# Rotary halves in separate chunks, scores of four heads in 32-row groups, and q and k by 512-column operands

## The chip, the cores and the metric

The kernel runs on one core of a Trainium2 chip. The metric is the device time of one execution in microseconds (us). The engines are PE (TensorE), ACT (ScalarE), DVE (VectorE), POOL (GpSimd) and SP, which issues the DMAs. PEld is the weight-load half of PE, which overlaps its matmuls.

## What is computed

Two layers of a decoder trunk on x of 256 tokens by 1024 channels. Each layer has three causal branches (a gated convolution of 31 taps, differential attention, block attention with one block), gates, an output projection, a layer norm and a squared-ReLU MLP. What the change touches is the rotary step and the scores of the two attentions:

```
u = x @ w_in[l]                                   # q and k of both attentions are column blocks of it
def apply_rope(x, cos, sin):                      # per head, 64 channels = two halves of 32
    x1, x2 = split(x, 2, axis=-1)
    return x * cos + concatenate([-x2, x1]) * sin
s = einsum("qd,kd->qk", q, k) * 64 ** -0.5        # per head; 8 heads in each attention, causal mask, softmax
```

The gates (`sigmoid(u_gate + b_gate)`) and the convolution (`conv_general_dilated` over 512 channels) run around these steps and share their engines.

## The kernel before

Every float32 operand is split in a high and a low float32r part, and a product is the sum of high by high, low by high and high by low. Weights come from HBM in **slabs** of 128 x 1024. For a slab, `Weights.get` (line 395) records a DMA into `raw`, a cast to `whi` on ACT and a subtraction that gives `wlo` on DVE; 4 raw and 8 whi/wlo buffers go round. x lies in `big` tiles, 256 columns of high and 256 of low part side by side, so that `x_both` is one 512-column operand.

A slab of the transposed projections holds 8 K chunks of 128 x 128 (`KT` = 8) and makes one chunk of 128 output channels over 256 tokens. There are two ways to multiply it:

- `tunit` (line 555; gates, and the MLP's first matrix with `hsplit`): for each K chunk one matmul of `whi` with the 512 columns of high and low x, then for each K chunk one of `wlo` with the 256 high columns. That is 8 matmuls of 512 and 8 of 256 columns. The two halves of the bank are then added by `tsum`: ACT copies the right half with the bias, DVE adds the left one.
- `qkunit` (line 575; q and k): `mm3` makes three matmuls of 256 columns for each K chunk, 24 for a slab, and two slabs fill one PSUM bank.

`rope` (line 655) takes such a bank: ACT makes four copies of 32 partitions that swap the halves of each head, DVE multiplies by cos, multiplies the swapped copy by a signed sin, and adds: three DVE instructions of 128 x 512. q or k of two slabs, which is four heads, is one unit; there are four q/k pairs of units in a layer (2 attentions by 2), 16 slabs, and 32 in the two layers.

`attn_scores` (line 675) makes the scores of two heads: for each head one matmul of 256 and one of 128 columns (the causal part) on 64 partitions, in float32, then mask and minimum on DVE and the exponential on ACT. It runs 8 times in a layer. Stages `d_a` to `d_d` (differential) and `m_a` to `m_c` (block attention) follow; `tick()` starts them after a given number of slabs.

PSUM has 8 banks (`BANKS`, line 30): 2 `pm` (projections), 4 `pa` (scores, transposes and products of the attention, layer norm), 2 `pt` (the second slab of `tunit`, some transposes).

The convolution is 124 **taps** in a layer, each one DVE instruction of 128 x 256 (`tap`, line 618; in the profile `big<-hpad,half,big`). All of them have to be done before `conv_ln` (line 810) transposes their sum on PE, in the third gate group.

The order on each engine comes from `Plan`: every operation is recorded with a cost, dependences and a latest time (`latest`, line 234), and `order` (line 286) then takes at each step the operation that can start first on its engine, and of those ready the one with the earliest latest time. Line 125 is the line in `record` that issues everything, so all groups in the profile carry it and are told apart by tile names. Taps have late times and fill the gaps on DVE.

Of the kernel before, what the change touches and what calls it, by code (L numbers as in the profile page):

```python
# [9 lines left out]
F32 = mybir.dt.float32  # L10
F32R = mybir.dt.float32r
AF = mybir.ActivationFunctionType
# [29 lines left out]
class Plan:  # L42
# [68 lines left out]
    def record(self, name, fn, method, args, kw):  # L111
# [253 lines left out]
def kernel(ctx: ExitStack, tc: tile.TileContext, x, xT, w_in, w_p2, w_o, w_f1, w_f2,  # L365
# [165 lines left out]
    for l in range(L):  # L531
# [23 lines left out]
        def tunit(ticks=True):  # L555
            out = []
            for c in range(2):
                w = W.get(k=KT)
                ps = bank(("pm", "pt")[c])
# [7 lines left out]
                if ticks:  # L567
                    tick()
            return out

        def tsum(dst, ps, bias):

            R.Activation.activation(dst, ps[:, SEQ:], AF.Identity, bias=bias)
            R.DVE.tensor_add(dst, dst, ps[:, 0:SEQ])

        def qkunit():
            ps = bank()
            for c in range(2):
                w = W.get(k=KT)
# [3 lines left out]
                tick()  # L583
            return ps
# [69 lines left out]

        def rope(ps, dst):
            qq = R.tile(work, [P, 1024], F32, "zz", 3)
            q, qr = qq[:, :512], qq[:, 512:]
            for a in range(0, P, 64):
                R.Activation.copy(qr[a:a + 32], ps[a + 32:a + 64])
                R.Activation.copy(qr[a + 32:a + 64], ps[a:a + 32])  # L660
            p3 = ps.rearrange("p (c n) -> p c n", c=2)
            q3 = q.rearrange("p (c n) -> p c n", c=2)
            qr3 = qr.rearrange("p (c n) -> p c n", c=2)
            cb = cosT.rearrange("p (o n) -> p o n", o=1).broadcast_to([P, 2, SEQ])
            sb = sinT.rearrange("p (o n) -> p o n", o=1).broadcast_to([P, 2, SEQ])
# [7 lines left out]
        def attn_scores(b, pair):  # L673

            q, k = [QK[b, w, pair // 2][:, pair % 2] for w in 'qk']
            pt = R.tile(work, [P, 2, 384], F32, "pt", 2)
            mn = col(4, "mn")
            ll = col(4, "ll")
            li = col(4, "li")
            for e in range(2):  # L680
# [4 lines left out]
                for (s, m, j) in ((slice(0, 256), slice(0, 256), 2 * e),  # L685
                                  (slice(256, 384), slice(128, 256), 2 * e + 1)):
                    R.DVE.tensor_tensor_reduce(
                        out=pt[:, e, s], in0=ps[:, s], in1=maskq[:, m], scale=-0.125,
                        scalar=3.0e38, op0=ALU.add, op1=ALU.min, accum_out=mn[:, j:j + 1])
                    R.Activation.activation(pt[:, e, s], pt[:, e, s], AF.Exp, bias=mn[:, j:j + 1],  # L690
                                         scale=-1.0, accum_out=ll[:, j:j + 1])
            R.DVE.reciprocal(li, ll)
            return pt, ll, li

        def transp(src):

            ps = bank("pa")
# [15 lines left out]
        def d_a(h):  # L713
            pt, ll, li = attn_scores(0, h)
# [17 lines left out]
        def d_c(h):  # L732
            t, li = state['d', h]
            ps = bank("pa")
# [18 lines left out]
        def d_d(h):  # L753
            o = state['d', h]
            ps = bank("pa")
# [5 lines left out]
        def m_a(j):  # L761
            pt, ll, li = attn_scores(1, j)
# [14 lines left out]
        def m_c(j):  # L777
            t = state['m', j]
            t = t.rearrange("p (e n) -> p e n", e=2)
            ps = bank("pa")  # L780
# [10 lines left out]
        jobs = [[lambda f=f, h=h: f(h) for f in (d_a, d_b, d_c, d_d)] for h in range(4)]  # L791
        jobs += [[lambda f=f, h=h: f(h) for f in (m_a, m_b, m_c)] for h in range(4)]
        start = [7, 9, 11, 14, 16, 18, 20, 22]
        ev = []
        for i, (j, s) in enumerate(zip(jobs, start)):
            for k, f in enumerate(j):
                ev.append((s + 3 * k, -k, i, f))
# [186 lines left out]
        for i in range(3, 16):  # L984
            do2(i - 3)
            ps = tunit()
# [24 lines left out]
def _layout(x, w_in, b_gate, conv_w, conv_b, conv_ln_g, conv_ln_b, w_conv_out,  # L1011
# [21 lines left out]
    for l in range(L):  # L1033
# [3 lines left out]
        for q, k in ((dq, dk), (mq, mk)):  # L1037
            a, b = tu(q), tu(k)
# [25 lines left out]
    sinT = np.concatenate([-s, s, -s, s])  # L1064
# [29 lines left out]
```

## Time and profile before

| | |
|---|---|
| median of 3 runs | 856.26 us (855.24 to 857.37) |
| the profiled execution's own time | 855.5 us |
| its span in the trace | 853.7 us |
| busy share: PE, DVE, ACT | 98%, 77%, 64% |
| mean granted PE clock | 0.996 |

The span goes from the first to the last instruction of the core; the 1.8 us between it and the execution's own time lie around it. A matmul's end in the trace is modelled and overlaps the next one, so times of PE are read from start to start. In the same way a DVE or ACT instruction overlaps the next by some 0.08 us; the time that one takes from a full queue is its start-to-start time.

### The profile page before, as it was taken

The numbers are of one execution on the slowest core, as the hardware profiler recorded it, in microseconds if no ns is written. First come the engines' busy times: TensorE is split into PE (matmuls) and PEld (weight loads), VectorE is DVE, ScalarE is ACT, GpSimd is POOL, SyncE is SP. The second block draws the span as 40 slices with busy tenths as digits, with TensorE's granted clock in tenths as the row PEclk, the third lists the DMA queues.
The fourth block names the chain that finished last, engine by engine and source line by source line (L and its number), as shares of the span: only waits on it lengthen the run. The fifth ranks groups of instructions, "written<-read, shape, count | busy, mean of one in ns | idle before, by whom it ended". The sixth has DMA issues, their size and how long they took to land.

```text
span 853.7 us, 13190 instructions
## 1 busy us (share of the span) xinstructions
PE 840.0 (98%) x4938; PEld 737.5 (86%) x4938; DVE 655.4 (77%) x1123; ACT 543.6 (64%) x916; POOL 18.0 (2%) x26
## 2 busy tenths in 40 slices
PE   9999999999999999999999999999999999999996
PEld 7899988889888888888888998898898788888885
DVE  6789999998797655555679999999787875555545
ACT  6568998557258666656454799966662586666650
POOL 0000010000000000000000001000000000000000
PEclk9999999999999999999999999999999999999999
DMA  9775424555548765555275743355643586565511
GB/s 342 284 249 166 138 89 136 196 187 188 194 148 271 272 197 194 179 194 195 77 233 176 241 152 113 102 172 171 202 163 129 207 301 214 193 196 197 195 52 50
DMA packets 44415, 156.95 MB, mean 184 GB/s; under 512 B 4928, under 2 KB 5696, under 8 KB 44352
## 3 DMA queue, kind: packets, MB, share of 16 engines
q1 hardware_dynamic: 43920, 155.60, 54.5%
q8 instruction: 38, 0.62, 0.3%
q10 hardware_dynamic: 432, 0.52, 0.2%
q14 instruction: 25, 0.20, 0.1%
HBM read 155.06 MB, written 1.05 MB: 183 GB/s over the span
## 4 chain that ended last, share of the span: by engine, by line
PE 88%; ACT 5%; DVE 4%; issue 1%; DMA 0%; POOL 0%; DVEq 0%; ACTq 0%
PE pm L125 41%; PE pa L125 31%; PE pt L125 16%; ACT zz L125 2%; DVE wlo L125 1%; ACT pt L125 1%; DVE big L125 1%; DVE zz L125 1%; ACT o L125 1%; DVE pt L125 1%; ACT whi L125 1%; DMA zz<-in_xT_dram 0%; DVE qk L125 0%; DVE col L125 0%; POOL col L125 0%
## 5 line engine op out<-in xcount | busy, mean ns | idle before, releaser
L125 DVE TENSOR_TENSOR wlo<-raw,whi 128x1024 fp32r<-128x1024 f32 (+1 forms) x282 | 341.0, 1214 | 135.6 <-ACT whi L125 133.9
L125 ACT CAST whi<-raw 128x1024 fp32r<-128x1024 f32 (+1 forms) x282 | 293.3, 1046 | 172.5 <-PE pm L125 56.2
L125 PE MATMUL pm<-big,whi 128*128 128x256 f32 (+1 forms) x1296 | 270.1, 320 | 0.0
L125 PEld LDWEIGHTS pm<-big,whi 128*128 128x128 f32 x1296 | 215.2, 191 | 17.2 <-DVE big L125 0.7
L125 PE MATMUL pa<-whi,big 128*128 128x512 f32 x704 | 217.6, 391 | 0.6 <-ACT whi L125 0.6
L125 PE MATMUL pm<-big,wlo 128*128 128x256 f32 x848 | 183.0, 283 | 0.0
L125 PEld LDWEIGHTS pa<-whi,big 128*128 128x128 f32 x704 | 130.0, 188 | 26.5 <-ACT whi L125 1.0
L125 PEld LDWEIGHTS pm<-big,wlo 128*128 128x128 f32 x848 | 141.1, 192 | 4.1
L125 PE MATMUL pa<-wlo,big 128*128 128x512 f32 x352 | 136.7, 390 | 0.0
L125 DVE SCALAR_TENSOR_TENSOR big<-hpad,half,big 128x256 f32<-128x256 f32 x240 | 103.3, 479 | 0.0
L125 PE MATMUL pt<-big,whi 128*128 128x512 f32 x400 | 101.2, 394 | 0.0
L125 PE MATMUL pm<-whi,big 128*128 128x512 f32 (+1 forms) x320 | 91.5, 371 | 0.0
L125 PEld LDWEIGHTS pt<-big,whi 128*128 128x128 f32 x400 | 71.9, 189 | 12.8
L125 PEld LDWEIGHTS pa<-wlo,big 128*128 128x128 f32 x352 | 66.1, 188 | 13.9
L125 PEld LDWEIGHTS pm<-whi,big 128*128 128x128 f32 x320 | 57.9, 189 | 10.4 <-ACT zz L125 0.4
L125 PE MATMUL pm<-wlo,big 128*128 128x512 f32 (+1 forms) x160 | 58.9, 370 | 0.0
L125 PEld LDWEIGHTS pt<-big,wlo 128*128 128x128 f32 x400 | 54.6, 190 | 3.9
L125 ACT ACTIVATE zz<-zz 128x512 f32<-128x512 f32 x58 | 36.7, 632 | 32.4 <-DVE zz L125 32.2
L125 PE MATMUL pt<-big,wlo 128*128 128x256 f32 x400 | 55.8, 282 | 0.0
L125 ACT COPY zz<-pm 32x512 f32<-32x512 f32 (+1 forms) x72 | 40.8, 566 | 6.8 <-DVE zz L125 3.8
L125 ACT ACTIVATE pt<-pt,col 128x256 f32<-128x256 f32 (+1 forms) x96 | 40.7, 453 | 1.0 <-DVE col L125 0.6
L125 PEld LDWEIGHTS pm<-wlo,big 128*128 128x128 f32 x160 | 30.1, 188 | 4.9
(88 smaller groups left out, 569.0 us busy)
## 6 DMA issues: line engine op xcount, KB each, us to landing
raw<-in_w_f_dram SPq DMA_DIRECT2D x128, 512.0 KB, 3.5
raw<-in_w_in_dram SPq DMA_DIRECT2D x110, 512.0 KB, 3.7
raw<-in_w_p_dram SPq DMA_DIRECT2D x24, 512.0 KB, 3.5
raw<-in_w_o_dram SPq DMA_DIRECT2D x16, 512.0 KB, 3.7
big<-in_rows_dram SPq DMA_DIRECT2D x10, 512.0 KB, 6.2
raw<-in_w_in_dram SPq DMA_DIRECT2D x4, 256.0 KB, 4.6
big<-in_x_dram SPq DMA_DIRECT2D x2, 512.0 KB, 7.0
out_dram<-big SPq DMA_DIRECT2D x4, 256.0 KB, 2.0
```

Source lines behind the costliest of these rows:

```text
L125: op.fn = lambda: fn(*args, **kw)
```

## The change

Six things change. The host lays out the q and k columns so that of two slabs the first has the first halves (32 channels) of four heads and the second has their second halves; sin has one sign. q and k go through `tunit`, 16 matmuls for a slab, and each slab has its own bank. `rope` starts with `tsum` of both slabs and then works between the chunks: one multiplication of 512 columns by cos, two of 256 by sin, one subtraction and one addition of 256. `attn_scores` makes four heads at once: each head has 32 partitions, and its score is the sum of two matmuls, one for each chunk, in its row group (`tile_position`). It runs 4 times in a layer and takes all four `pa` banks. The transposes and products of the attention move from `pa` to `pt`, and the gates move from `pm`/`pt` to two `pm` banks (the default of `tunit`); the MLP keeps `pm`/`pt`. The planner's cost of a PE operation is scaled by its rows and columns, and the stages have new start ticks.

```diff
+            op.cost *= ins[0].ap[0][1] / P * (main.ap[0][1] / P if method == "matmul" else 1)
-        def tunit(ticks=True):
+        def tunit(tags=("pm", "pm")):
...
-                ps = bank(("pm", "pt")[c])
+                ps = bank(tags[c])
...
         def tsum(dst, ps, bias):
-            R.Activation.activation(dst, ps[:, SEQ:], AF.Identity, bias=bias)
+            if bias is None:
+                R.Activation.copy(dst, ps[:, SEQ:])
+            else:
+                R.Activation.activation(dst, ps[:, SEQ:], AF.Identity, bias=bias)
             R.DVE.tensor_add(dst, dst, ps[:, 0:SEQ])
-        def qkunit():
-            ps = bank()
-            for c in range(2):
-                w = W.get(k=KT)
-                for kt in range(KT):
-                    mm3(ps[:, c * 256:(c + 1) * 256], at(w, ALLP, kt), x_at(X, kt), kt == 0,
-                        kt == KT - 1)
-                tick()
-            return ps
...
         def rope(ps, dst):
+            for c in range(2):
+                tsum(dst[:, c * SEQ:(c + 1) * SEQ], ps[c], None)
...
-            for a in range(0, P, 64):
-                R.Activation.copy(qr[a:a + 32], ps[a + 32:a + 64])
-                R.Activation.copy(qr[a + 32:a + 64], ps[a:a + 32])
...
             R.DVE.tensor_mul(q3, p3, cb)
-            R.DVE.tensor_mul(qr3, qr3, sb)
-            R.DVE.tensor_add(dst, q, qr)
+            for c in range(2):
+                R.DVE.tensor_mul(qr3[:, c], p3[:, 1 - c], sinT)
+            R.DVE.tensor_sub(d3[:, 0], q3[:, 0], qr3[:, 0])
+            R.DVE.tensor_add(d3[:, 1], q3[:, 1], qr3[:, 1])
...
-        def attn_scores(b, pair):
+        def attn_scores(b, u):
...
-                r = slice(64 * e, 64 * e + 64)
-                R.PE.matmul(ps[:, 0:256], q[r, 128:256], k[r], start=True, stop=True)
-                R.PE.matmul(ps[:, 256:384], q[r, 0:128], k[r, 0:128], start=True, stop=True)
+            ps = [bank("pa") for _ in range(4)]
+            for cols, qs, ks in ((slice(0, 256), slice(128, 256), slice(0, 256)),
+                                 (slice(256, 384), slice(0, 128), slice(0, 128))):
+                for c in range(2):
+                    for e in range(4):
+                        r = slice(32 * e, 32 * e + 32)
+                        R.PE.matmul(ps[e][:, cols], q[r, c, qs], k[r, c, ks], start=c == 0,
+                                    stop=c == 1, tile_position=(32 * e, 0))
...
-            ps = bank("pa")
+            ps = bank("pt")
...
-                    ps = qkunit()
+                    ps = tunit()
...
-            ps = tunit()
+            ps = tunit(("pm", "pt"))
             hsplit(i, ps)
...
-            a, b = tu(q), tu(k)
+            a, b = [tu(v.reshape(D, 2, 4, 2, 32).transpose(0, 1, 3, 2, 4).reshape(D, 512))
+                    for v in (q, k)]
...
-    sinT = np.concatenate([-s, s, -s, s])
+    sinT = np.concatenate([s, s, s, s])
```

Two places in the order are needed below. The first is PE at the first scores of layer 0, before; `pm` and `pa` are PSUM tiles, `qk` the rotated q and k, and `whi`, `wlo` and `big` the parts of weights and x.

```order
L125 MATMUL pm_186<-big_78,wlo_189 128x256
L125 MATMUL pm_186<-big_78,whi_188 128x256
L125 MATMUL pa_194<-qk_175,qk_166 128x256
L125 MATMUL pa_194<-qk_175,qk_166 128x128
L125 MATMUL pa_195<-qk_175,qk_166 128x256
L125 MATMUL pa_195<-qk_175,qk_166 128x128
L125 MATMUL pm_186<-big_75,whi_199 128x256
```

The same place after; of the 16 score matmuls the first eight and the ninth stand here, and the other seven are 128 columns wide like the ninth.

```order
L125 MATMUL pm_192<-big_78,wlo_191 128x256 x2
L125 MATMUL pa_193<-qk_177,qk_167 128x256
L125 MATMUL pa_194<-qk_177,qk_167 128x256
L125 MATMUL pa_195<-qk_177,qk_167 128x256
L125 MATMUL pa_196<-qk_177,qk_167 128x256
L125 MATMUL pa_193<-qk_177,qk_167 128x256
L125 MATMUL pa_194<-qk_177,qk_167 128x256
L125 MATMUL pa_195<-qk_177,qk_167 128x256
L125 MATMUL pa_196<-qk_177,qk_167 128x256
L125 MATMUL pa_193<-qk_177,qk_167 128x128
```

One set of four heads has taken the place of two sets of two, and the four row groups follow each other in turn.

The second place is DVE at the end of layer 0's convolution, before. `big<-big,pm` and `big<-big,pt` are the additions of `tsum` in the gates, `big<-hpad,half,big` are taps (the rows here hold the last ones), and `wlo` is the low part of a slab.

```order
L125 SCALAR_TENSOR_TENSOR big_94<-hpad_93,half_18_91,big_94 128x256 x2
L125 TENSOR_TENSOR wlo_453<-raw_451,whi_452 128x1024
L125 SCALAR_TENSOR_TENSOR big_94<-hpad_93,half_18_91,big_94 128x256
L125 TENSOR_TENSOR big_429<-big_429,pm_433 128x256
L125 SCALAR_TENSOR_TENSOR big_94<-hpad_93,half_18_91,big_94 128x256 x5
L125 TENSOR_TENSOR big_429<-big_429,pt_437 128x256
L125 TENSOR_TENSOR wlo_470<-raw_468,whi_469 128x1024
L125 TENSOR_TENSOR wlo_474<-raw_472,whi_473 128x1024
```

The same place after, on DVE; the `BN_STATS` row reads the bank into which `conv_ln` transposes the taps' sum.

```order
L125 TENSOR_TENSOR big_437<-big_437,pm_449 128x256
L125 SCALAR_TENSOR_TENSOR big_94<-hpad_93,half_18_91,big_94 128x256 x4
L125 TENSOR_TENSOR wlo_457<-raw_455,whi_456 128x1024
L125 TENSOR_TENSOR big_437<-big_437,pm_453 128x256
L125 SCALAR_TENSOR_TENSOR big_94<-hpad_93,half_18_91,big_94 128x256 x4
L125 TENSOR_TENSOR wlo_461<-raw_459,whi_460 128x1024
L125 SCALAR_TENSOR_TENSOR big_94<-hpad_93,half_18_91,big_94 128x256 x8
L125 TENSOR_TENSOR big_454<-big_454,pm_458 128x256
L125 TENSOR_TENSOR wlo_478<-raw_476,whi_477 128x1024
L125 TENSOR_TENSOR big_454<-big_454,pm_462 128x256
L125 BN_STATS cst_392_465<-pa_464 128x6
```

The taps have moved back: before, the last one stands in front of the second addition of the third gate group, four slabs ahead of the transposes of `conv_ln`; after, the last one stands in front of that group's fifth addition, and the transposes follow the sixth slab.

## Rows read from the trace of the kernel before

**Rows 1.** The page's busy time by engine (share of span) and count of instructions

```profile
PE 840.0 (98%) x4938; PEld 737.5 (86%) x4938; DVE 655.4 (77%) x1123; ACT 543.6 (64%) x916; POOL 18.0 (2%) x26
```

**Rows 2.** Timeline, PE in a q/k slab: start, length, engine, line, operation, out<-in, shapes

```profile
60.78 0.28 PE L125 MATMUL pm<-big,wlo 128*128 128x256 f32 x1
60.90 0.28 PE L125 MATMUL pm<-big,whi 128*128 128x256 f32 x1
```

**Rows 3.** Timeline, PE in the gates: the starts of two slabs that follow each other

```profile
182.64 2.00 PE L125 MATMUL pt<-big,whi 128*128 128x512 f32 x8
...
185.44 2.00 PE L125 MATMUL pm<-big,whi 128*128 128x512 f32 x8
```

**Rows 4.** Timeline, PE at the first scores of layer 0

```profile
70.62 0.28 PE L125 MATMUL pm<-big,whi 128*128 128x256 f32 x1
70.83 0.93 PE L125 MATMUL pa<-qk,qk 64*128 64x256 f32 x8
71.69 0.39 PE L125 MATMUL pm<-big,whi 128*128 128x256 f32 x1
71.91 0.28 PE L125 MATMUL pm<-big,wlo 128*128 128x256 f32 x1
```

**Rows 5.** Timeline, PE: score matmuls in flight together at three instants, 70.885, 71.325, 71.655

```profile
70.83 0.49 PE L125 MATMUL pa<-qk,qk 64*128 64x256 f32 x2
...
71.15 0.39 PE L125 MATMUL pa<-qk,qk 64*128 64x256 f32 x2
...
71.48 0.28 PE L125 MATMUL pa<-qk,qk 64*128 64x128 f32 x2
```

**Rows 6.** Timeline, PE: the two score pairs that waited, and what followed them

```profile
111.29 0.92 PE L125 MATMUL pa<-qk,qk 64*128 64x256 f32 x4
...
113.70 0.50 PE L125 MATMUL pm<-big,whi 128*128 128x512 f32 x1
...
529.89 0.92 PE L125 MATMUL pa<-qk,qk 64*128 64x256 f32 x4
...
532.52 0.73 PE L125 MATMUL pm<-big,whi 128*128 128x512 f32 x2
```

**Rows 7.** Windows of layer 1: us, busy by engine (instructions), granted clock, DMA share, GB/s

```profile
532.00:534.00 2.00, 2.00 (x9) 1.57 (x8) 2.00 (x10) 2.00 (x5) 0.00 (x0) 0.79 0.00 0
534.00:535.00 1.00, 1.00 (x4) 0.81 (x3) 1.00 (x6) 1.00 (x5) 0.00 (x0) 0.50 0.00 0
535.00:536.00 1.00, 1.00 (x5) 0.81 (x5) 1.00 (x2) 1.00 (x6) 0.00 (x0) 0.50 0.00 0
536.00:537.00 1.00, 1.00 (x8) 1.00 (x8) 0.64 (x3) 0.06 (x1) 0.00 (x0) 0.71 0.29 66
```

**Rows 8.** Groups by form: count | busy, mean ns | idle before, released by

```profile
L125 ACT COPY zz<-pm 32x512 f32<-32x512 f32 x64 | 37.0, 578 | 4.9 <-DVE zz L125 3.8
```

**Rows 9.** Timeline, DVE in the q/k stage: the rotary sum, a slab's low part, the next

```profile
62.10 0.69 DVE L125 TENSOR_TENSOR qk<-zz 128x512 f32<-128x512 f32 x1
62.70 1.22 DVE L125 TENSOR_TENSOR wlo<-raw,whi 128x1024 fp32r<-128x1024 f32 x1
63.84 0.69 DVE L125 TENSOR_TENSOR zz<-pm,cst 128x512 f32<-128x512 f32 x1
```

**Rows 10.** Timeline, ACT and DVE in the gates: the two halves of tsum

```profile
182.84 0.48 ACT L125 ACTIVATE big<-pm,cols 128x256 f32<-128x256 f32 x1 [0.26 <-PE pm L125]
183.35 0.42 DVE L125 TENSOR_TENSOR big<-big,pm 128x256 f32<-128x256 f32 x1
...
186.57 0.42 DVE L125 TENSOR_TENSOR big<-big,pt 128x256 f32<-128x256 f32 x1
186.91 1.22 DVE L125 TENSOR_TENSOR wlo<-raw,whi 128x1024 fp32r<-128x1024 f32 x1
```

**Rows 11.** Timeline, layer 0: DVE's last five taps; PE's first transposes of conv_ln

```profile
178.10 2.06 DVE L125 SCALAR_TENSOR_TENSOR big<-hpad,half,big 128x256 f32<-128x256 f32 x5
...
191.03 1.03 PE L125 MATMUL pa<-cst,big 128*128 128x128 f32 x8
```

More of the change, by code (lines that the diff above doesn't have):

```diff
@@ L670 @@
+            R.DVE.tensor_sub(d3[:, 0], q3[:, 0], qr3[:, 0])
+            R.DVE.tensor_add(d3[:, 1], q3[:, 1], qr3[:, 1])
         QK = {}
         o_sb = {}
-        def attn_scores(b, pair):
[L675 to L680, printed above, removed]
-                ps = bank("pa")
-                r = slice(64 * e, 64 * e + 64)
-                R.PE.matmul(ps[:, 0:256], q[r, 128:256], k[r], start=True, stop=True)
-                R.PE.matmul(ps[:, 256:384], q[r, 0:128], k[r, 0:128], start=True, stop=True)
[L685 to L693, printed above, removed]
@@ new lines, in attn_scores @@
+        def attn_scores(b, u):
+            q, k = [QK[b, w, u] for w in 'qk']
+            ps = [bank("pa") for _ in range(4)]
[6 more added lines that the diff above has]
+                                    stop=c == 1, tile_position=(32 * e, 0))
+            res = []
+            for i in range(2):
+                pt = R.tile(work, [P, 2, 384], F32, "pr", 2)
+                mn = col(4, "mn")
+                ll = col(4, "ll")
+                li = col(4, "li")
+                for e in range(2):
+                    for (s, m, j) in ((slice(0, 256), slice(0, 256), 2 * e),
+                                      (slice(256, 384), slice(128, 256), 2 * e + 1)):
+                        R.DVE.tensor_tensor_reduce(
+                            out=pt[:, e, s], in0=ps[2 * i + e][:, s], in1=maskq[:, m],
+                            scale=-0.125, scalar=3.0e38, op0=ALU.add, op1=ALU.min,
+                            accum_out=mn[:, j:j + 1])
+                        R.Activation.activation(pt[:, e, s], pt[:, e, s], AF.Exp,
+                                             bias=mn[:, j:j + 1], scale=-1.0,
+                                             accum_out=ll[:, j:j + 1])
+                R.DVE.reciprocal(li, ll)
+                res.append((pt, ll, li))
+            return res
@@ L695, in transp @@
         def transp(src):
-            ps = bank("pa")
+            ps = bank("pt")
             R.PE.transpose(ps[:, 0:128], src[:, 256:384], ident)
@@ L711, in branch, with d_a @@
             return BR[b]
-        def d_a(h):
-            pt, ll, li = attn_scores(0, h)
+        def d_a(h, sc):
+            pt, ll, li = sc
             cc = col(2, "cc")
@@ L733, in d_c @@
             t, li = state['d', h]
-            ps = bank("pa")
+            ps = bank("pt")
             hs = slice(h * 128, (h + 1) * 128)
@@ L754, in d_d @@
             o = state['d', h]
-            ps = bank("pa")
+            ps = bank("pt")
             R.PE.transpose(ps[:, 0:128], o[:, 128:256], ident)
@@ L758, in d_d, with m_a @@
             split(*at(branch(0), ALLP, h), ps[:, 0:256], subg)
-        def m_a(j):
-            pt, ll, li = attn_scores(1, j)
+        def m_a(j, sc):
+            pt, ll, li = sc
             for e in range(2):
@@ L779, in m_c @@
             t = t.rearrange("p (e n) -> p e n", e=2)
-            ps = bank("pa")
+            ps = bank("pt")
             for k, (c0, c1) in enumerate(((0, 256), (256, 384))):
@@ L789, in m_c, with scores @@
                 split(*at(branch(1), r, j), ps[r, e * 256:(e + 1) * 256])
-        jobs = [[lambda f=f, h=h: f(h) for f in (d_a, d_b, d_c, d_d)] for h in range(4)]
-        jobs += [[lambda f=f, h=h: f(h) for f in (m_a, m_b, m_c)] for h in range(4)]
-        start = [7, 9, 11, 14, 16, 18, 20, 22]
+        def scores(b, u):
+            for i, sc in enumerate(attn_scores(b, u)):
+                (d_a, m_a)[b](2 * u + i, sc)
         ev = []
-        for i, (j, s) in enumerate(zip(jobs, start)):
-            for k, f in enumerate(j):
-                ev.append((s + 3 * k, -k, i, f))
+        for b, u, t in ((0, 0, 7), (0, 1, 12), (1, 0, 18), (1, 1, 24)):
+            ev.append((t, 0, 2 * b + u, lambda b=b, u=u: scores(b, u)))
+            for i in range(2):
+                for k, f in enumerate(((d_b, d_c, d_d), (m_b, m_c))[b]):
+                    ev.append((t + i + 3 * k + 4, -k, 2 * b + u,
+                               lambda f=f, h=2 * u + i: f(h)))
         for e in sorted(ev, key=lambda e: e[:3]):
```

7 lines of the change are left out of this document (3 added, 4 removed).

## The prediction, made before the changed kernel was run

> **What bounds the kernel now.** I read the page first. PE is busy for 98% of the span [rows 1], and the chain of waits runs over PE for nearly all of its length, so a change counts by what it takes from PE or makes PE wait. The next question is how fast PE goes within its busy time, since a matmul's end is modelled: I read starts from the timeline. Where PE does not go at its pace, the waits and the granted clock tell why. Last I looked at DVE in the stretch from the q/k slabs to the convolution's end, because the order shows that the change puts work there.
>
> **Part 1: q and k by 512 columns.** A q/k slab now is 24 matmuls of 256 columns that start 0.12 us apart [rows 2], 2.88 us. A slab in the gates has the form that q and k get, 8 of 512 and 8 of 256 columns, and the next slab starts 2.80 us after it [rows 3]. The columns are the same, 6144, so only 0.08 us goes, for 8 fewer instructions. For 32 slabs: **-2.6 us**, all on PE, with little doubt.
>
> **Part 2: four heads at once.** A pair of heads now costs PE this: the last slab matmul starts at 70.62 and would be followed 0.12 later; the slab goes on at 71.69, and its first matmul takes 0.22 instead of 0.12 [rows 4]. That is 0.95 + 0.10 = 1.05 us, and 16 pairs cost 16.8. Inside, the two heads run side by side in their 64-row groups: two matmuls are in flight in each of three instants [rows 5]. Each group makes, for one head, two records of 256 columns and two of 128 (8 records in all). A start gap of 0.33 (71.48 - 71.15) covers a 256 and a 128 record, so two of each take 0.65 of streaming, and 0.40 of the 1.05 is entering and leaving. After the change each row group makes twice as many records, since a head's sum comes from two chunks. If four groups run side by side as the two do, a set of four heads takes 2 x 0.65 + 0.40 = 1.70, and 8 sets take 13.6: **-3.2 us**. No row shows four groups. The bounds are one stream wide open (1.70) and two at a time (2 x 1.30 + 0.40 = 3.0, 24.0 in all, +7.2 against now). I take 1.70, as the two groups did not cost each other anything.
>
> The Trainium skill (page "TensorE: Matmul & The Clock Gate", section "Measured speedup vs the span model") says that four row groups of 32 with 512 columns gave 3.07 times, not 4. By that the streaming is an estimated 1.30 x 4 / 3.07 = 1.69 us, and the gain of this part falls by about 3.1 us. No run here shows it yet; it has a rival below.
>
> **Part 3: the two pairs that waited.** In each layer one pair stood still in its middle for a `pa` bank that ACT had to empty: from 111.29 to 113.70 and from 529.89 to 532.52 [rows 6], 2.41 and 2.63 us where an undisturbed pair takes 0.86 (70.83 to 71.69, [rows 4]). That is 1.55 + 1.77 = 3.3 us. After the change `pa` holds nothing but scores until the convolution's norm, and its four banks are free when a set starts; ACT also loses the four copies of a unit, 4 x 0.58 us [rows 8], for two of 256 columns that are at most a 0.48 `tsum` activation each [rows 10]. So I take both waits as gone, **-3.3**. What is late next there is the `pt` bank of the transposes, which now shares two banks; its chain has one slab of 2.80 between users and I count nothing.
>
> **Part 4: the clock.** Right after the second wait the granted clock falls from 2.4 to 1.2 GHz: 0.79, 0.50, 0.50 and 0.71 in windows of 2, 1, 1 and 1 us [rows 7]. PE lost 0.42 + 0.50 + 0.50 + 0.29 = 1.7 us. It had stood still and made little in the 3 us ahead of the fall. With the wait gone I take the fall as gone: **-1.7**, and zero as the other end.
>
> **Part 5: DVE.** Start to start, a 512-column sum takes 0.60 and a slab's low part 1.14 [rows 9], a 256-column sum 0.34 [rows 10], a tap (2.06 - 0.08) / 5 = 0.40 [rows 11]. `rope` was 3 x 0.60 = 1.80 for a unit and becomes 6 x 0.34 + 0.60 = 2.64 (two `tsum` sums, two by sin, two last ones; one by cos): +0.84, for 8 units **6.7 us more DVE work in a layer**. In the q/k stage the planner pays for it by pushing taps back, so it comes due before `conv_ln`. Now the last tap ends at 180.16 and PE begins its transposes at 191.03 [rows 11]: 10.9 us of cover. PE comes earlier by what parts 1 to 3 give up to there in layer 0 (1.3 + 1.6 + 1.6 = 4.5), DVE later by 6.7 at least. The cover is gone, to within 0.3 us, before any idle time of DVE.
>
> Idle time there will be, as the queue is in order and the additions of `tsum` wait for PE. So I count the end in the new order. From the fourth addition of the second gate group to the last tap there are 40 taps, 6 low parts and 7 additions: wait-free 40 x 0.40 + 6 x 1.14 + 7 x 0.34 = 25.2 us. That first addition starts 0.71 us after its slab ends (183.35 - 182.64, [rows 3, 10]), so the last tap ends 25.9 us after it. PE has 8 slabs of 2.80 in that time, 22.4. PE waits **+3.5 us** in layer 0. In layer 1 the same count leaves a pile only at the end: 11 taps, a low part and an addition are 5.9, with 0.71 it is 6.6 against two slabs of 5.6: **+1.0**. The bounds are 0 (DVE ran ahead before that stretch) and, above, the whole extra work of both layers, 13.4.
>
> The two `pm` banks of the gates come in here too. Now four banks go round; with two, an addition that ends more than 2.80 - 0.71 - 0.34 = 1.75 us late stops PE. In the stretch just counted the additions grow late by up to 2.3, so part of the 3.5 will be seen as waits for `pm` before the transposes. It is the same time and isn't counted twice. In the q/k stage a unit has 2 x 1.14 + 2.64 = 4.9 us of DVE work against 5.6 of PE, within the cover: 0.
>
> A wait of 3.5 us is longer than the one ahead of the fall in part 4, so I give a fall of the clock there half a chance at the same price: **+0.9**.
>
> **Sum.** -2.6 - 3.2 - 3.3 - 1.7 + 3.5 + 1.0 + 0.9 = -5.4 us. The profiled execution took 855.5 (span 853.7), so 850.1. The median of the three runs lies 0.8 above that execution; between the two I say **850.4 us**, and 847 to 854 for this case's own range.
>
> **Rivals.**
> A, the forecast: 850.4.
> B, four row groups cost each other something: if they run at the rate of three, the streaming is 1.30 x 4 / 3 = 1.73, +0.43 for each of 8 sets, 853.9. For it: four accumulating streams where the trace shows two. Against: [rows 5]. (The Trainium skill's 3.07 from the page above gives almost the same, 853.5.)
> C, two groups at a time: +1.30 for each set, 850.4 + 10.4 = **860.8, slower than before**. Place: the 8 score sets, on PE. It decides if PE can hold only two row groups open. Against it: two groups start together today though one stands behind the other in the queue.
> D, DVE and the two banks set the pace of the gates: from the fourth slab on, the new order has 4 x 0.40 + 1.14 + 0.34 = 3.08 us of DVE work (4 taps, a low part and an addition) for a slab of 2.80. If that holds for all 48 gate slabs, it is 48 x 0.28 = 13.4 in place of the 4.5 + 0.9, and with one fall of the clock it is 850.4 - 5.4 + 13.4 + 1.7 = 860.1. It decides once an addition is over 1.75 late early in a stage. Against: layer 1's counts mostly stay below 2.80.
> E, DVE is ahead when the stretch begins and no wait comes: 850.4 - 5.4 = 845.0.
>
> **How the numbers follow.** A measurement of this kernel can tell about 0.3% from no change, so the bounds are 853.7 and 858.8. A has 0.50 (0.44 of it faster, 0.06 within), B 0.12 (0.05 faster, 0.07 within), C 0.08 (slower), D 0.17 (0.08 within, 0.09 slower), E 0.13 (faster). Together faster 0.62, within 0.21, slower 0.17. The range goes from E to D, 844.5 to 860, and leaves out C and the tails.
>
> **What would show it.** q/k slabs that start 2.80 apart. A set of scores that takes 1.70 from slab to slab, with four matmuls in flight; 3.0 would be C. No wait of PE on ACT at the scores, and the clock at full there. A wait of 3 to 4 us on DVE at layer 0's `conv_ln` or just ahead of it, and about 1 in layer 1; if it is spread over many gate slabs, it is D. The forecast is wrong if the waits of part 3 come back at the `pt` banks, or if q/k slabs wait for a `pm` bank.

## The result, and the profile after

| | before | after |
|---|---|---|
| median, 7 runs each | 855.38 us | 858.93 us |
| ratio, 95% interval | | 1.0053 (1.0038 to 1.0067) |
| the profiled execution and its span | 855.5, 853.7 us | 860.1, 858.3 us |
| the likeliest case of the prediction | | 850.4 us |

The changed kernel is half a per cent slower. The forecast was 0.6 per cent faster. The page's busy times after, to be read beside [rows 1]:

```profile
PE 839.0 (98%) x4810; PEld 722.7 (84%) x4810; DVE 666.6 (78%) x1187; ACT 517.2 (60%) x884; POOL 17.8 (2%) x26
```

PE has 128 matmuls fewer, DVE is busy 11 us more and ACT 26 us less. Cutting the two spans at the same points of the program (the first score matmul of a layer, the first transpose of `conv_ln`, the first matmul of the output projection `w_o`) shows where the 4.6 us between them lie:

| stretch | before | after | difference |
|---|---|---|---|
| start to the first scores of layer 0 | 70.8 | 70.3 | -0.6 |
| scores to `conv_ln`, layer 0 | 120.2 | 119.1 | -1.1 |
| `conv_ln` to `w_o`, layer 0 | 30.4 | 31.4 | +1.0 |
| `w_o` of layer 0 to the first scores of layer 1 | 268.1 | 276.3 | **+8.2** |
| scores to `conv_ln`, layer 1 | 122.6 | 116.4 | -6.2 |
| `conv_ln` to `w_o`, layer 1 | 30.4 | 31.3 | +1.0 |
| `w_o` of layer 1 to the end | 211.3 | 213.5 | **+2.2** |

The stretches that the prediction worked out came near it; the ones for which it had no term lost over 10 us. The wait view of the whole span has these rows (the tile that PE was to write, the engine and tile that it waited for, us in total, times, longest):

```profile
PE pa L125 <- DVE big L125: 6.5, 3, 2.9
PE pa L125 <- ACT zz L125: 1.8, 2, 1.2
...
PE pt L125 <- DVE zz L125: 0.9, 1, 0.9
PE pm L125 <- DVE wlo L125: 0.5, 2, 0.4
PE pm L125 <- DVE qk L125: 0.3, 1, 0.3
```

Two of the three waits for `big` are at the start of `w_o`, and they are the same in both layers. Timeline of PE there, layer 0 and then layer 1:

```profile
220.79 1.09 PE L125 MATMUL pa<-whi,big 128*128 128x512 f32 x4
224.74 0.80 PE L125 MATMUL pa<-whi,big 128*128 128x512 f32 x1 [2.85 <-DVE big L125]
...
230.79 0.40 PE L125 MATMUL pa<-wlo,big 128*128 128x512 f32 x1
...
648.73 0.50 PE L125 MATMUL pa<-whi,big 128*128 128x512 f32 x1 [2.85 <-DVE big L125]
...
652.04 0.39 PE L125 MATMUL pa<-wlo,big 128*128 128x512 f32 x1
```

PE made four matmuls that need only high parts and then stood still for the low part of M, the sum of the branches. DVE in layer 0 at that time:

```profile
221.66 0.68 DVE L125 SCALAR_TENSOR_TENSOR big<-big,pm 128x512 f32<-128x512 f32 x1
222.26 0.69 DVE L125 TENSOR_TENSOR big<-big,big 128x512 f32<-128x512 f32 x1
222.86 1.22 DVE L125 TENSOR_TENSOR wlo<-raw,whi 128x1024 fp32r<-128x1024 f32 x1
224.00 0.69 DVE L125 SCALAR_TENSOR_TENSOR big<-big,big 128x512 fp32r<-128x512 f32 x1
```

The row at 224.00 is the first low part of M; PE goes on when it ends. In the kernel before, the same instruction started at 217.44, four us ahead of `w_o`:

```profile
217.44 0.69 DVE L125 SCALAR_TENSOR_TENSOR big<-big,big 128x512 fp32r<-128x512 f32 x1 [0.33 <-ACT big L125]
```

The clock fell during the wait in layer 0 and not in layer 1. Windows (us, busy by engine, granted clock):

```profile
223.80:230.70 6.90, 5.96 (x14) 4.72 (x15) 6.90 (x10) 2.62 (x3) 0.00 (x0) 0.51 0.72 250
...
646.00:649.00 3.00, 0.27 (x1) 0.27 (x2) 3.00 (x5) 2.17 (x3) 0.00 (x0) 1.00 0.43 147
```

The clock stood at 1.2 GHz for 6.8 us, but PE stood still in the first 0.9 of them. What the fall cost is read from the 14 matmuls behind the wait: 6.05 us in layer 0 (224.74 to 230.79) and 3.31 in layer 1 (648.73 to 652.04), where the clock held, so 2.7 us. (The expectations below take it at 3.4, half of its length.) So 2.85 + 2.7 of the 8.2 in that stretch are this one wait and its fall. Waits at the two layer norms behind it (1.19 and 0.91), where the kernel before had none in layer 0, and 0.31 at a q/k slab are most of the rest. In the last stretch the same wait of 2.85 came, and the norm behind it waited 0.57 where it had waited 1.63 before.

### The profile page after: what moved, and what is told of

Read it like the earlier page. It is cut to its first block, busy times and chain, and to the rows that moved or that the text cites. A ratio compares the mean times of both kernels' runs of the same rounds, so it can differ in the third digit from the quotient of the medians.

```text
span 858.3 us, 12905 instructions
## 1 busy us (share of the span) xinstructions
PE 839.0 (98%) x4810; PEld 722.7 (84%) x4810; DVE 666.6 (78%) x1187; ACT 517.2 (60%) x884; POOL 17.8 (2%) x26
## 4 chain that ended last, share of the span: by engine, by line
PE 92%; DVE 5%; DMA 1%; ACT 1%; issue 1%; DVEq 0%; ACTq 0%
PE pm L125 49%; PE pa L125 30%; PE pt L125 12%; DVE big L125 3%; DVE wlo L125 2%; DMA raw<-in_w_in_dram 1%; ACT whi L125 1%; ACT zz L125 0%; DVE zz L125 0%; DVE st L125 0%; DVEq L1101 0%; ACT big L125 0%; DVE qk L125 0%; DVE col L125 0%; ACT qk L125 0%
## 5 line engine op out<-in xcount | busy, mean ns | idle before, releaser
L125 PE MATMUL pm<-big,whi 128*128 128x512 f32 (+1 forms) x1232 | 288.4, 362 | 0.3 <-DVE qk L125 0.3
L125 PEld LDWEIGHTS pm<-big,whi 128*128 128x128 f32 x1232 | 213.8, 189 | 31.4 <-DVE big L125 0.7
L125 PE MATMUL pa<-whi,big 128*128 128x512 f32 x704 | 220.4, 395 | 5.7 <-DVE big L125 5.7
L125 PE MATMUL pm<-big,wlo 128*128 128x256 f32 x1040 | 172.8, 283 | 0.5 <-DVE wlo L125 0.5
L125 PEld LDWEIGHTS pm<-big,wlo 128*128 128x128 f32 x1040 | 152.1, 190 | 10.4 <-DVE wlo L125 2.2
L125 PE MATMUL pt<-big,whi 128*128 128x512 f32 x208 | 52.4, 392 | 0.0
L125 ACT ACTIVATE pr<-pr,col 128x256 f32<-128x256 f32 (+1 forms) x96 | 40.6, 447 | 8.4 <-DVE col L125 8.3
L125 PEld LDWEIGHTS pt<-big,whi 128*128 128x128 f32 x208 | 37.4, 189 | 6.6
L125 ACT ACTIVATE big<-pm,cols 128x256 f32<-128x256 f32 x48 | 22.8, 474 | 29.8 <-PE pm L125 29.6
L125 DVE TENSOR_TENSOR big<-zz,big 128x512 fp32r<-128x512 f32 (+1 forms) x37 | 25.0, 677 | 12.3 <-ACT big L125 12.3
L125 ACT CAST big<-pt 128x256 fp32r<-128x256 f32 (+1 forms) x40 | 13.3, 376 | 33.4 <-PE pt L125 33.3
```

The costliest lines, as they stand in the source:

```text
L125: op.fn = lambda: fn(*args, **kw)
```

## Experiments

Four theories were in play. WORK, later DEBT: the rotary step gives DVE 6.7 us more work in a layer, and PE pays for it at the norm and again behind it. ORDER: the planner's new cost of PE operations puts DVE's queue in a bad order. BANKS: two banks for the gates are too few. CHAIN, later QUEUE: only the place of M's first part in the queue matters. "The norm" is `conv_ln` here, unless a layer norm is named.

**Less convolution.** The last 17 taps of one chunk are not made.

```diff
-            for k in range(TAPS):
+            for k in range(TAPS if c < 3 else TAPS - 17):
```

> The changed kernel without the last 17 taps of the convolution's fourth chunk in each layer (107 in place of 124; that part of the convolution is left out): 17 x 0.40 = 6.8 us less DVE work in a layer, about what the new rotary step adds (6.7). Theory WORK (the time is lost because DVE has 6.7 us more to do in a layer, and PE pays at the convolution's norm and again at the output projection): the waits of 2.85 us at the output projection of both layers and the fall of the clock after the first go, and most of the waits at the norm: 858.9 - 13 = 846 us, within 843 to 849. Theory ORDER (the planner's new PE cost puts taps and low parts in a worse order on DVE, and the amount of work matters little): the order still ends the taps at the same gate slab, so the waits stay for the larger part: 853 us or more.

Measured 848.68 us, ratio to before 0.9927 (0.9912 to 0.9941). Taking DVE's extra work away gave 10.2 us. In its profile PE does not wait at the norm, nor at `w_o` of layer 1, and the clock does not fall. A wait of 2.2 us stays at `w_o` of layer 0:

```profile
PE pa L125 <- DVE big L125: 2.2, 1, 2.2
```

For WORK, with that remainder open.

**q and k by three matmuls.** The part of the change that brought `tsum` into the rotary step is undone; the rest stays.

```diff
-                    ps = tunit()
+                    ps = qkunit()
...
-            for c in range(2):
-                tsum(dst[:, c * SEQ:(c + 1) * SEQ], ps[c], None)
-            p3 = dst.rearrange("p (c n) -> p c n", c=2)
+            p3 = ps.rearrange("p (c n) -> p c n", c=2)
```

> The changed kernel with q and k again by three matmuls of 256 columns for each K chunk, both chunks in one bank, and the rotary step read from that bank, so without the two copies and two additions of a unit: DVE 2 x 0.34 x 8 = 5.4 us less in a layer, PE 0.08 x 32 = 2.6 us more in all. WORK: four fifths of what the waits and the fall cost come back, 858.9 + 2.6 - 11 = 850.5 us, within 847 to 854. ORDER: the planner's cost stays, so 858.9 + 2.6 = 861.5 us, within 857 to 863.

Measured 853.90 us, ratio 0.9993 (0.9984 to 1.0003), at the upper end of WORK. The waits at the norms went, and the one at `w_o` of layer 1 fell to 0.5 us; that of layer 0 stayed at 2.8, and 3.4 us at 1.2 GHz followed it. The 512-column operands, worth 2.6 us of PE time, cost more through DVE than they save.

**Without the planner's new cost.**

```diff
-            op.cost *= ins[0].ap[0][1] / P * (main.ap[0][1] / P if method == "matmul" else 1)
```

> The changed kernel without the line that scales the planner's cost of a PE operation by its rows and columns; same instructions, other order: on DVE 91 taps in place of 62 lie ahead of the ninth addition of the gates in layer 0, and 7 low parts in place of 13 between the convolution's norm and the output projection. WORK: DVE has as much to do, so PE waits as much, only earlier (rotary steps and additions of the q/k stage come late): 856 to 861 us. ORDER: the waits at the norm and at the output projection go, and the fall of the clock: 846 to 850 us.

Measured 866.35 us, ratio 1.0136 (1.0119 to 1.0153): outside both ranges, 7.4 us slower than with the line. PE's waits:

```profile
PE pm L125 <- DVE big L125: 6.7, 11, 1.4
PE pm L125 <- DVE qk L125: 5.8, 4, 1.7
```

With the taps further ahead, PE waits for rotary sums and additions instead, and more. ORDER as stated falls: the line is a gain within this change. The debt can be paid early or late, and early was dearer.

**The kernel before with more DVE work.**

```diff
             R.DVE.tensor_mul(qr3, qr3, sb)
+            R.DVE.tensor_mul(dst, q, qr)
+            R.DVE.tensor_mul(dst[:, 0:128], q[:, 0:128], qr[:, 0:128])
             R.DVE.tensor_add(dst, q, qr)
```

> The kernel before with two more DVE instructions in each rotary unit (a product of 512 and one of 128 columns into the result tile, overwritten by the sum behind them): 0.60 + 0.21 = 0.81 us a unit, 6.5 us in a layer, near the 6.7 that the change adds, with the old matmuls, scores, banks and planner's cost. WORK: PE pays for most of what 10.9 us of cover and the stock of low parts do not hide, 2 to 5 us in a layer: 860 to 866 us against 855.4. ORDER: within 2 us of the kernel before, 854 to 857 us.

Measured 858.56 us, ratio 1.0042 (1.0026 to 1.0057), between the two ranges. The old kernel too pays for the work, 3.7 us for 13, less than WORK's range, and in part in the same place: a wait of 1.6 us came at `w_o` of layer 0, and the longest wait for ACT at the scores grew from 0.9 to 1.9. That it pays less because its PE comes later (to `conv_ln` at 193.89, where the changed kernel comes at 189.40) is argued, not shown.

**Four banks for the gates.**

```diff
-                ps = tunit()
+                ps = tunit(("pm", "pt"))
```

> The changed kernel with the gates on pm and pt again, four banks in turn, as in the kernel before. Theory DEBT (DVE has 6.7 us more to do in a layer and pays it in two places, at the convolution's norm and at the output projection, where the stock of low parts made ahead is gone): the banks only move the first wait, 856 to 860 us against 858.9 for the changed kernel. Theory BANKS (additions that come late stop PE since only two banks go round): the slow slabs ahead of the norm in layer 0 (0.26 to 0.65 us over 2.79) and what follows from them go, 852 to 855 us.

Measured 858.61 us, ratio 1.0044 (1.0028 to 1.0061), the same as the changed kernel. In its profile the waits ahead of the norm are gone and those at `w_o` stay at 2.8 and 2.3, with 3.4 us at 1.2 GHz at each. But PE came later to the gates ahead of the norm, by 2.5 us for the same slab. The changed kernel, then this run:

```profile
172.91 2.00 PE L125 MATMUL pm<-big,whi 128*128 128x512 f32 x8
```

```profile
175.45 2.00 PE L125 MATMUL pt<-big,whi 128*128 128x512 f32 x8
```

The same matmuls, from the first scores to `conv_ln`, take 118.8 and 118.1 us in the two layers, against 119.1 and 116.4. So PE lost ahead of these slabs what it no longer waited in them; why is open. BANKS falls as it was stated.

**The products by sin on POOL.** In this run and the next the planner's cost of a POOL operation also goes by its columns.

```diff
-                R.DVE.tensor_mul(qr3[:, c], p3[:, 1 - c], sinT)
+                R.Pool.tensor_tensor(qr3[:, c], p3[:, 1 - c], sinT, op=ALU.mult)
```

> The changed kernel with the two products by sin of each rotary unit on POOL in place of DVE: 2 x 0.34 x 8 = 5.4 us less DVE work in a layer, as in the run with q and k by three matmuls, but without its 2.6 us more on PE. DEBT: 853.9 - 2.6 = 851.3 us, within 848 to 854, if POOL takes under 1.5 us for one and DVE keeps its pace beside it. BANKS: only the debt of DVE matters little, 856 us or more. If POOL's work slows DVE as much as it takes from it: 857 to 861.

Measured 856.90 us, ratio 1.0034 (1.0021 to 1.0047): 2 us better than the changed kernel, where 7.6 were expected. DVE does not keep its pace beside POOL. An instruction of POOL, and the product by cos that DVE started while it ran; then a product by cos that kept its time, while POOL's two instructions there took 3.36 us:

```profile
64.88 0.92 POOL L125 TENSOR_TENSOR zz<-qk,cst 128x256 f32<-128x256 f32 x1 [2.96 <-DVE qk L125]
...
65.12 1.23 DVE L125 TENSOR_TENSOR zz<-qk,cst 128x512 f32<-128x512 f32 x1
...
71.36 3.36 POOL L125 TENSOR_TENSOR zz<-qk,cst 128x256 f32<-128x256 f32 x2 [2.62 <-DVE qk L125]
...
71.60 0.68 DVE L125 TENSOR_TENSOR zz<-qk,cst 128x512 f32<-128x512 f32 x1
```

The 16 products by cos took 0.69 us on average in the changed kernel and 0.93 here.

**Low parts of `w_o` on POOL.**

```diff
-            plan.DVE.tensor_sub(lo[:, s], raw[:, s], hi[:, s].bitcast(F32))
+            if i % 140 in (69, 71, 73, 75):
+                plan.Pool.tensor_tensor(lo[:, s], raw[:, s], hi[:, s].bitcast(F32), op=ALU.subtract)
+            else:
+                plan.DVE.tensor_sub(lo[:, s], raw[:, s], hi[:, s].bitcast(F32))
```

> The changed kernel with the low parts of four of the eight slabs of each layer's output projection on POOL: 4 x 1.14 = 4.6 us less DVE work between the convolution's norm and the end of the projection, and nothing changed ahead of the norm. DEBT: the waits of 2.85 us at the start of both projections go, with them the fall of the clock in layer 0 (3.4 us), while the waits at the norm stay: 858.9 - 5.7 - 3.4 = 849.8 us, within 848 to 853. A rival, CHAIN (the projection waits for the sums of the branches, whatever low parts stand between): 857 us or more. If POOL is so slow that PE waits for its low parts: over 859.

Measured 869.33 us, ratio 1.0175 (1.0159 to 1.0192). It tells nothing of DEBT, since DVE was not relieved: POOL's instruction and the DVE sum that ran into it, and the same sum undisturbed.

```profile
213.94 2.39 POOL L125 TENSOR_TENSOR wlo<-raw,whi 128x1024 fp32r<-128x1024 f32 x1 [16.28 <-ACT whi L125]
...
214.18 2.70 DVE L125 TENSOR_TENSOR big<-big,big 128x512 f32<-128x512 f32 x1
...
217.94 0.68 DVE L125 TENSOR_TENSOR big<-big,big 128x512 f32<-128x512 f32 x1
```

The waits at `w_o` grew to 6.0 and 5.6 us.

**The same low parts left out.**

```diff
-        lo = plan.tile(self.pool, [P, 1024], F32R, "wlo", NW)
+        skip = i % 140 in (69, 71, 73, 75)
+        lo = hi if skip else plan.tile(self.pool, [P, 1024], F32R, "wlo", NW)
...
+            if not skip:
+                plan.DVE.tensor_sub(lo[:, s], raw[:, s], hi[:, s].bitcast(F32))
```

> The changed kernel without the low parts of four of the eight slabs of each layer's output projection (they are left out, and the matmuls that would read them read the high part again, so that PE has the same work): 4 x 1.14 = 4.6 us less DVE work between the convolution's norm and the end of the projection, with no other engine in their place. DEBT: the two waits of 2.85 us at the start of the projections go, with the fall of the clock in layer 0 (3.4 us); the waits at the norm stay: 858.9 - 5.7 - 3.4 = 849.8 us, within 848 to 853. CHAIN (the projection waits for the sums of the branches, whatever low parts stand between): 857 us or more.

Measured 853.55 us, ratio 0.9985 (0.9974 to 0.9996). Both waits at `w_o` fell from 2.85 to 0.45 and the clock held, while the wait at layer 0's norm stayed (0.77, as in the changed kernel). The three are in one row:

```profile
PE pa L125 <- DVE big L125: 1.7, 3, 0.8
```

That is DEBT, half a us above its range: the waits did not go all the way, and the layer norm behind still waits 0.8 in each layer. CHAIN falls.

**Another due time for M.** The sums of the last two branch projections and the parts of M are due 30 us earlier.

```diff
+                    R.bias = -30000
                     R.DVE.scalar_tensor_tensor(g, in0=g, scalar=1.0, in1=ps, op0=ALU.add, op1=ALU.mult)
                     R.DVE.tensor_add(a, a, g)
...
+                    R.bias = 0.0
```

> The changed kernel with the same instructions, and the sums of the last two branch projections and the parts of M made from them given an earlier due time (30 us) in the planner: on DVE 9 low parts in place of 13 stand between the convolution's norm and the first low part of M, and that one stands ahead of the last slab's sum in place of behind it. DEBT (what counts is how much DVE has to make up by the end of the output projection): the wait only moves from M to the low parts of the projection's later slabs, 856 to 860 us. QUEUE (DVE would have the time, but the first part of M stands behind the last sum and a low part in its queue, 2.85 us each time): both waits go, and the fall of the clock in layer 0: 858.9 - 5.7 - 3.4 = 849.8 us, within 848 to 853.5 (the same cut by less DVE work gave 853.6). Between these, 853.5 to 856: some of both.

Measured 864.68 us, ratio 1.0086 (1.0065 to 1.0108), outside both ranges. PE did not wait at the start of `w_o`. But the new order had PE do both token halves of `w_o` together, and PE then stood still behind the layer norm, in both layers, with 6.8 us at 1.2 GHz each. Layer 0:

```profile
244.36 1.32 PE L125 MATMUL pt<-cst,big 128*128 128x128 f32 x8 [1.06 <-DVE big L125]
246.10 0.62 PE L125 MATMUL pm<-whi,big 128*128 128x512 f32 x2 [0.41 <-ACT big L125]
250.01 0.79 PE L125 MATMUL pm<-whi,big 128*128 128x512 f32 x1 [3.30 <-DVE big L125]
```

**The same, with PE's old order kept.**

```diff
+            if t == 0:
+                last = R.ops[-1]
+            else:
+                for o in R.ops[-6 * KT:]:
+                    o.deps.setdefault(last, False)
+                    last.succ.append(o)
             ln_tok(t, ps, xtok[t], ALPHA, gb1, xtok[t], X)
```

> The run before it (the sums and the parts of M due earlier) with one more rule for the planner: in the output projection all matmuls of the first 128 tokens come before those of the second, as they do in the kernel before. Same instructions and the same DVE work as in the changed kernel. In the run before it the waits at the start of the projection were gone, but PE did both token halves together and then stood still for 3.3, 1.1 and 0.4 us at the layer norm, with a fall of the clock in each layer. QUEUE (DVE has the time, the changed kernel only has the first part of M behind the last sum in its queue): no wait of more than 1 us at the projection nor at the norm behind it and no fall: 858.9 - 5.7 - 3.4 = 849.8 us, within 848.5 to 853. DEBT (with the first half alone PE wants eight low parts in 11 us, while DVE has eight of 1.14 and ten sums and parts of 0.60 ahead of the last one, 15 us): PE waits 2 to 4 us for low parts in the projection of each layer, 856 to 861 us.

Measured 861.29 us, ratio 1.0067 (1.0043 to 1.0090), just above DEBT's range. M comes in time, and PE waits inside `w_o` for weights:

```profile
PE pa L125 <- ACT whi L125: 4.1, 2, 2.3
...
PE pa L125 <- DVE wlo L125: 1.5, 2, 0.9
```

Low parts that are late hold the `raw` buffers, so the next slabs' high parts are late too: in layer 0 the DMAs of the last two slabs of `w_o` start at 226.32 and 228.06, each under 0.1 us after a low part ended, and land at 232.1 and 233.6; ACT makes their high parts then. The wait moves, it does not go. QUEUE falls: M's first part came early in both runs and neither got faster.

**The cost line alone, in the kernel before.**

```diff
+            op.cost *= ins[0].ap[0][1] / P * (main.ap[0][1] / P if method == "matmul" else 1)
```

> The kernel before with the line alone that scales the planner's cost of a PE operation: same instructions, other order; 12 and 9 low parts in place of 8 and 7 stand between the convolution's norm and the output projection on DVE. DEBT: DVE has no more to do than before, and its order only shifts a little idle time: 853 to 857 us. A rival, LINE (the new cost moves the taps back further than DVE can make good, whatever its work): a wait of 1.5 to 2.5 us at the output projection of layer 0 with a fall of the clock, 858 us or more.

Measured 853.36 us, ratio 0.9985 (0.9973 to 0.9998), in DEBT's range. The rival LINE was right about the wait, but no fall followed it and the time did not grow. The run shows two more things. The waits for ACT at the scores [rows 6] and the fall [rows 7] are gone although the banks are the old ones, so a better order takes them away by itself. And a wait of 2.2 us comes at `w_o` of layer 0, with the old amount of work. So the remainder in the run with fewer taps belongs to the order that this line makes: it moves taps back, and with them low parts behind the norm, as more work does. At layer 0's `w_o` the line alone makes 2.2 of the 2.85 us; in layer 1 it makes none.

**Fewer DVE additions in the gates.** q and k by three matmuls as above, and for three gate groups the same, with the tanh taken straight from the bank.

```diff
+                if bi < 2 - l:
+                    ps = qkunit()
...
+                        R.Activation.activation(g[:, s], ps[:, s], AF.Tanh,
+                                                bias=half[:, n:n + 1], scale=0.5)
```

> The run with q and k by three matmuls (853.9 us), and in the first two gate groups of layer 0 and the first of layer 1 the gates by three matmuls of 256 columns too: ACT then takes its tanh straight from the bank, the additions of 24 slabs go from DVE (8.0 us in all), and PE pays 24 x 0.08 = 1.9 us. DEBT: the waits at the output projection, about 2.8 + 0.5 us, and the fall of the clock (1.7) go, with some of those at the layer norms (0.5 to 1): 853.9 + 1.9 - 5.5 = 850.3 us, within 848.5 to 852.5, faster than both kernels. Without DEBT: 855 us or more.

Measured **849.83 us, ratio 0.9938 (0.9918 to 0.9957)**, faster than both kernels, as expected. No wait at the norm or at `w_o` is left, and none on DVE is over 0.8 us but the one at the start of the program (`mhalf`):

```profile
PE pt L125 <- DVE mhalf L125: 1.2, 1, 1.2
PE pt L125 <- DVE zz L125: 0.8, 1, 0.8
PE pt L125 <- issue: 0.6, 1, 0.6
PE pa L125 <- ACT zz L125: 0.3, 1, 0.3
```

**All gates so** (the condition is always true).

> As the run before it, but with all gates of both layers by three matmuls: 48 additions, 16 us of DVE work, less than in the run with q and k by three matmuls, and PE pays 48 x 0.08 = 3.8 us. DEBT: nothing is left to gain behind the run before it, so only PE's 1.9 us more come on top: 852.2 us, within 850.5 to 854.

Measured 850.77 us, ratio 0.9944 (0.9924 to 0.9965), in its range: 0.9 us above the run before it, where PE's price was 1.9. Once DVE keeps up, taking more additions from it gains nothing in total.

Over the runs in which neither POOL, work at `w_o` nor due times were touched, the wait at `w_o` grows with one count, the low parts that DVE has to make between the second `BN_STATS` of `conv_ln` and the first low part of M (from the order, layer 0 / layer 1; the waits from the traces):

| kernel | low parts | wait at `w_o`, us |
|---|---|---|
| before | 8 / 7 | 0 / 0 |
| without the planner's new cost (its waits come earlier) | 7 / 7 | 0 / 0 |
| all gates; three gate groups | 10 / 8; 10 / 9 | 0 / 0 |
| before with more work | 11 / 10 | 1.6 / 0 |
| fewer taps; cost line alone | 12 / 10; 12 / 9 | 2.2 / 0 |
| q and k by three matmuls | 13 / 11 | 2.8 / 0.5 |
| four banks | 13 / 13 | 2.8 / 2.3 |
| after | 13 / 13 | 2.85 / 2.85 |

The two layers do not lie on one line: 11 go with 1.6 us in layer 0 and with 0.5 in layer 1.

## Why the prediction was wrong, by its own steps

**Part 1 held.** q/k slabs start 2.79 to 2.80 apart. What the part left out of its price is what the 512-column form needs behind it: the additions on DVE were counted in part 5, and there not to their end.

**Part 2 held.** A set of four heads costs 1.71 us by the same reckoning as before, against 1.70. Rows at the first set, two instants with all four groups in flight:

```profile
70.27 1.59 PE L125 MATMUL pa<-qk,qk 32*128 32x256 f32 x32
71.02 0.39 PE L125 MATMUL pa<-qk,qk 32*128 32x256 f32 x4
71.23 0.40 PE L125 MATMUL pa<-qk,qk 32*128 32x128 f32 x8
71.78 0.73 PE L125 MATMUL pm<-big,whi 128*128 128x512 f32 x2
```

The last slab matmul starts at 70.06, so 71.78 - 70.06 - 0.12 = 1.60, and the first matmul of the next slab takes 0.10 longer. From 71.02 to 71.23 four records of 256 columns, one in each group, take 0.21 us, what one group's record takes in [rows 5]. The 3.07-fold speedup for four row groups in the Trainium skill ("TensorE: Matmul & The Clock Gate", section "Measured speedup vs the span model") would make this set an estimated 2.1 us; the trace does not agree, as the set took 1.71: here the four groups cost each other nothing. Rivals B and C fall.

**Parts 3 and 4 came out, and the reason given is not the only one that does it.** PE waits for ACT at no score set, and the clock holds there. The prediction put that down to free `pa` banks and a relieved ACT; the run with the cost line alone has neither and lost the waits too, and the run without that line, which has both, has none either. Which of them did it in the changed kernel is open.

**Part 5 is the step that failed.** Its waits at the norm were near: 3.5 us forecast in layer 0, and measured 0.43 + 0.26 + 0.65 + 1.20 in the slabs and 0.73 in the transposes, 3.3; in layer 1 1.0 forecast and 0.6 measured. Where the profile names a releaser, it is a low part of the weights or the taps, not a `pm` bank:

```profile
175.70 2.00 PE L125 MATMUL pm<-big,whi 128*128 128x512 f32 x8
177.86 1.22 PE L125 MATMUL pm<-big,wlo 128*128 128x256 f32 x8 [0.16 <-DVE wlo L125]
178.92 2.00 PE L125 MATMUL pm<-big,whi 128*128 128x512 f32 x8
...
181.97 2.00 PE L125 MATMUL pm<-big,whi 128*128 128x512 f32 x8
184.37 1.21 PE L125 MATMUL pm<-big,wlo 128*128 128x256 f32 x8 [0.39 <-DVE wlo L125]
185.41 2.00 PE L125 MATMUL pm<-big,whi 128*128 128x512 f32 x8
187.42 1.22 PE L125 MATMUL pm<-big,wlo 128*128 128x256 f32 x8
189.40 1.63 PE L125 MATMUL pa<-cst,big 128*128 128x128 f32 x8 [0.76 <-DVE big L125]
```

But the account was closed there. The prediction took the 10.9 us between the last tap and the transposes [rows 11] for cover, as if DVE were free in them. It was not: it made low parts for slabs to come, seven of them between the last tap and the norm's `BN_STATS`. After the change there is one. What was pushed out had to be made behind the norm, and the first half of `w_o`, 11 us, wants eight slabs. The windows show it (the third busy time is DVE's): from the first q/k slab to `conv_ln`, to `w_o`, and to the layer norm, before and then after.

```profile
50.60:191.00 140.40, 139.70 (x997) 127.80 (x996) 134.43 (x302) 110.99 (x236) 4.08 (x5) 1.00 0.49 162
191.00:221.40 30.40, 30.40 (x243) 29.73 (x242) 26.72 (x43) 19.58 (x29) 1.10 (x2) 1.00 0.59 189
221.40:244.10 22.70, 22.70 (x107) 18.83 (x106) 16.73 (x26) 7.41 (x11) 0.97 (x1) 1.00 0.39 130
```

```profile
50.60:189.40 138.80, 137.47 (x934) 119.56 (x933) 131.45 (x321) 94.45 (x217) 3.89 (x4) 1.00 0.45 146
189.40:220.80 31.40, 31.40 (x241) 29.81 (x242) 29.92 (x48) 20.47 (x29) 1.30 (x3) 1.00 0.63 208
220.80:249.40 28.60, 25.75 (x106) 20.79 (x105) 22.30 (x35) 10.50 (x15) 0.97 (x1) 0.88 0.44 154
```

Up to the norm DVE did 3.0 us less than before, although it had 6.7 more to do; behind the norm it did 3.2 + 5.6 = 8.8 us more, in a stretch that PE's wait and the fall made longer. That is the missing term, which the prediction had at nothing: 2.85 us at each `w_o` and 2.7 for the fall; the layer norms' waits grew by 1.0 in all beside it. The fall was given half a chance, at the norm and at 1.7 us; it came at `w_o` and cost 2.7. Not all of it is the new work: in layer 0 the planner's line alone puts 12 low parts behind the norm in place of 8 and makes a wait of 2.2 us, while in layer 1 it takes the line and the work together.

**The rivals.** D had the right engine and, at 860.1, the nearest time, but the wrong mechanism: the gates of layer 1 run at 2.80, and four banks do not change the time. Its price was the whole extra work plus a fall, which is about what PE paid. E falls with the waits at the norm. The range held the time only because D's price was its upper end, and as D's mechanism did not happen, that was luck. The sign of the likeliest case was wrong, since a debt of 13 us of DVE work was priced at 4.5.

**What stays open**: whether some order of the same instructions hides the backlog. None of the three tried did (866.35, 864.68 and 861.29 us).

## What to carry to other kernels

Where an engine prepares data ahead of the one that sets the time, its time between two deadlines is not cover just because no deadline falls in it: count what it makes there for later, and follow the debt to the next burst of demand. An operand form that saves PE 0.08 us a slab and costs 0.34 on the engine in second place is worth its price only as long as that engine has slack; here the reverse trade, three matmuls in place of an addition, was the gain. And once order has been tried, taking work away from the late engine is what paid.

## What the runs showed of the hardware

**POOL and DVE block each other.** A DVE product that started within a POOL product of 256 columns (0.92 us) took 1.23 us in place of 0.68, and a DVE sum within a POOL subtraction of 2.39 us took 2.70 in place of 0.68. The other way round, a POOL product that started at 58.44, within a low part on DVE (58.28 to 59.50), took 1.66 us. The Trainium skill ("Trainium Architecture — The Big Picture", section "What this means for kernel authors") calls the port that the two share an exclusive lock; these rows agree. So an idle POOL was no spare capacity for work on SBUF.

**The same wait did not always bring the clock down.** A wait of 2.85 us at `w_o` brought 6.8 us at 1.2 GHz in layer 0 and none in layer 1 of one execution; two waits of 2.2 us (fewer taps; the cost line alone) were followed by none, and one of 1.8 us (with the old order kept) by 3.4 us. A fall behind such a wait is priced from both ends, 0 and the 2.7 us that the first of these cost.
